# Causal mask in the scan's second term, VectorE's remainders and sums one step later, softmax values loaded three steps later: an encoder layer on one core

## The chip, the core and the metric

The kernel runs on one NeuronCore of a Trainium2 chip. Its engines work side by side and wait for each other by semaphores: TensorE (PE, with its weight loads shown apart as PEld), VectorE (DVE), ScalarE (ACT), GpSimd (POOL), and SyncE (SP), which here issues nearly all transfers between the on-chip memory and HBM. TensorE writes only into eight accumulator banks (PSUM), each 128 rows by 512 float32. The metric is the device time of one execution in microseconds (us).

## What is computed

One layer of an encoder over 2048 positions of width 1024, all in float32: a projection, two kinds of attention with 8 heads of 64 each, an output projection, and a squared-ReLU MLP. The change touches the two attentions only.

```python
# stick-breaking heads: strictly causal
z = einsum(q, k) * scale
strict = s_idx < t_idx
log_beta = log_sigmoid(z)
log_1m_beta = where(strict, log_sigmoid(-z), 0.0)
suffix = cumsum(log_1m_beta, reverse=True) - log_1m_beta
w = where(strict, exp(log_beta + suffix), 0.0)
out = einsum(w, v)
...
# softmax heads: own chunk of 64 and the 8 before it, with a bias by distance
p = softmax(einsum(q, k_band) * scale + bias)
out = einsum(p, v_band)
```

The sequence is stored reversed, so the keys that a query may see stand to its right, and the reverse cumulative sum becomes a running product from left to right.

## The kernel before

The kernel has three stages: projections of the first positions (to about 423 us of the profile), attention (to about 1357 us), and the rest of the output projection and the MLP. To keep TensorE busy in the attention stage, the remaining projections and most of the output projection are fed in between as *filler*: `fill` takes some of their matmuls in each step by a credit. Their results are split and stored by jobs in the list `soon`, which the next step runs as `done` (`stf`, `svf` and `xr` are tiles of such jobs).

**Units and steps.** Positions are cut into four groups g of 512. For g = 3, 2, 1, 0 come first the stick-breaking units `SB(h, g, c)`, head h and key group c from g to 3, then the softmax units `CA(h, g)`. A unit has four steps, one for each block of 128 queries. A unit with c equal to g is *diagonal*: its rows get shorter (512, 384, 256, 128 keys). In step i the loop works on a front unit (scores and weights) and on the unit of eight steps before (LAG), the back unit, whose weights are transposed and multiplied with the values. The names below carry head, groups and block: `p_2_2_3_0` is head 2, g 2, c 3, block 0 of a stick-breaking unit; `v_0_2` has two numbers and is head 0, g 2 of a softmax unit.

**One step, in the order of the code.** TensorE transposes one or two 128-key blocks of the back unit (`wt`); `soft1` of the front unit; `parts` (ScalarE rounds wt to `wth`, VectorE subtracts to get the remainder `wtl`: a float32 product is made of rounded parts); `soft2`; the jobs of `done`; the matmuls of values `acc` with wth and wtl of a block three back (AVLAG); the scores `z` (softmax: `cz`, `ct`) of the next step; filler. In `soft1` of a stick-breaking unit ScalarE makes sigmoid(z) in `b` and sigmoid(-z) in z, VectorE scans z into the running product `p`, and GpSimd multiplies b with p, shifted by one. The scan computes p[j+1] = z[j] * p[j] + second[j]; its second operand is a zero repeated over the row. Scores, transposes share four accumulator banks (`pz`), so a score matmul waits until the scan of an earlier score has read its bank.

**The mask.** In a diagonal unit, a third matmul adds -1e30 to the first 128 score columns where the key is not visible (`identb`, `maskb`, in bf16, 1 LDWEIGHTS and 1 matmul). The sigmoids then give 0 and 1 there.

**End of a head.** `finish` has ScalarE copy one half of the accumulator to `otmp`, VectorE add the other half into `o`; after each second head `keep` splits o into `os` and stores it to `scr_m`.

**Loads.** All go through SP's one queue, in its order. At a unit's first step, q, k and (softmax) the bias of the unit two ahead are issued (AHEAD); a unit's values `v` are issued when its own step 2 comes (VST). A softmax v has two buffers, its bias two, so an issue can wait in SP's queue until the buffer's last reader is done. `fw`, `fv`, `fx` and `ow` are the filler's loads. TensorE's order is that of the code; of the other engines a scheduling layer may move independent instructions, so the built program's order is shown below.

Nearly every row of the profile has line L42, the wrapper through which instructions are handed on; rows are told apart by their tiles.

Of the kernel before, what the change touches and what calls it, by code (L numbers as in the profile page):

```python
# [18 lines left out]
P = 128  # L19
S = 2048  # L20
D = 1024
HD = 64
# [57 lines left out]
def encoder_kernel(ctx, tc, xT, c, g1, g2, w_in, w_rest, gqk, bias, w_o, w1, w2, w_ada, b_ada, out):  # L80
# [20 lines left out]
    def scratch(name, shape, *counts):  # L101
# [12 lines left out]

    ident = cpool.tile([P, P], F32, name="ident")
    make_identity(nc, ident)
    identb = cpool.tile([P, P], BF16, name="identb")
    dve.tensor_copy(identb, ident)
    maskb = cpool.tile([P, P], BF16, name="maskb")
    pool.memset(maskb, 0.0)  # L120
    pool.affine_select(
        out=maskb, in_=maskb, pattern=[[1, P]], base=0, channel_multiplier=-1,
        compare_op=ALU.is_gt, fill=NEG,
    )
    ones = cpool.tile([P, P], F32, name="ones")
    pool.memset(ones, 1.0)
    zero = cpool.tile([P, 1], F32, name="zero")
# [19 lines left out]
    def split(hi, lo, src, lo_eng=None):  # L147
        act.copy(hi, src)
        (lo_eng or dve).tensor_tensor(lo, src, hi.bitcast(F32), op=ALU.subtract)
# [503 lines left out]
    if True:  # L653
# [36 lines left out]
        def finish(u):  # L690
            r = (u.h % 2) * HD
            q = HD - r
            if u.h % 2 == 0:
                pend["o"] = op.tile([P, TB], F32, tag="o", name=f"o{u.nm}")
            o = pend["o"]
            tmp = op.tile([P, TB], F32, tag="otmp", name=f"otmp{u.nm}")
            act.copy(tmp[r : r + HD, :], u.acc[q : q + HD, :])
            dve.tensor_tensor(o[r : r + HD, :], u.acc[r : r + HD, :], tmp[r : r + HD, :], op=ALU.add)
            if u.h % 2:
                soon.append(lambda: keep(u, o))  # L700

        def keep(u, o):

# [9 lines left out]
        class Unit:  # L713
# [13 lines left out]
                    pe.transpose(wt[:, qi * P : (qi + 1) * P], self.weights(qi, kb), ident)  # L727
                self.wt[j] = wt

            def parts(self, j):  # L730
                kb, q0, q1 = self.blocks[j]
                nm = f"{self.nm}_{kb}"
                wt = self.wt[j]
                wh = wtp.tile([P, TB], F32R, tag="wth", name=f"wth{nm}")
                wl = wtp.tile([P, TB], F32R, tag="wtl", name=f"wtl{nm}")
                cols = slice(q0 * P, q1 * P)
                split(wh[:, cols], wl[:, cols], wt[:, cols])
                self.wt[j] = (wh, wl, cols, kb)

            def values(self, j):  # L740
# [10 lines left out]
        class SB(Unit):  # L751
# [21 lines left out]
            def scores(self, qi):  # L773
                nm = f"{self.nm}_{qi}"
                c0 = qi * P if self.diag else 0
                n = TB - c0
                self.z = z = pz.tile([P, TB], F32, tag="z", name=f"z{nm}")
                qs = slice(qi * P, (qi + 1) * P)
                pe.matmul(z[:, :n], self.q[:, 0, qs], self.k[:, c0:], start=True, stop=False)
                pe.matmul(z[:, :n], self.q[:, 1, qs], self.k[:, c0:], start=False, stop=not self.diag)  # L780
                if self.diag:
                    pe.matmul(z[:, :P], identb, maskb, start=False, stop=True)

            def soft1(self, qi):
                nm = f"{self.nm}_{qi}"
                c0 = qi * P if self.diag else 0
                n = TB - c0
                z = self.z
                b = zw.tile([P, TB], F32, tag="w", name=f"b{nm}")
                pt = zp.tile([P, TB + 1], F32, tag="p", name=f"p{nm}")  # L790
                act.activation(b[:, :n], z[:, :n], AF.Sigmoid, scale=0.125)
                act.activation(z[:, :n], z[:, :n], AF.Sigmoid, scale=-0.125)
                before = ones[:, 0:1] if self.diag else self.carry[qi]
                pool.tensor_copy(pt[:, 0:1], before)
                dve.tensor_tensor_scan(
                    pt[:, 1 : n + 1], z[:, :n], zero.to_broadcast([P, n]), 1.0 if self.diag else before,
                    op0=ALU.mult, op1=ALU.add,
                )
                pool.tensor_tensor(b[:, :n], b[:, :n], pt[:, :n], op=ALU.mult)
                self.carry[qi] = pt[:, n : n + 1]  # L800
                self.ws.append((b, c0))
# [304 lines left out]
        weight = STEPS * sum(u.weight for u in units) + LAG * 0.6  # L1106
        credit = 0.0
        rest = 0
        late, soon, first = [], [], []

        def fill(part, more=0):

# [37 lines left out]
        def value(u, j):  # L1150
            u.values(j)

        VST = 2
        AHEAD = 2
        for u in units[:AHEAD]:
            load(u)
# [9 lines left out]
        pado.tile([P, 80], F32, tag="pad", name="pado")  # L1166
        fp = ph.enter_context(tc.tile_pool(name="fp", bufs=3))
        wtp = ph.enter_context(tc.tile_pool(name="wtp", bufs=4))
        ldq = sp
        steps = [(u, st) for u in units for st in range(STEPS)]  # L1170

        turns = {STEPS * n: 4 if u.ca else 8 for n, u in enumerate(units) if n and u.ca != units[n - 1].ca}
        for i in range(len(steps) + LAG):
            if i % STEPS == 0:
                if i // STEPS + AHEAD < len(units):
                    load(units[i // STEPS + AHEAD])
            vi = i - VST
            if vi >= 0 and vi % STEPS == 0 and vi // STEPS < len(units):
                units[vi // STEPS].load_values()
            front, fs = steps[i] if i < len(steps) else (None, 0)  # L1180
            back, bs = steps[i - LAG] if i >= LAG else (None, 0)
            done = list(soon)
# [4 lines left out]
                js = range(nb * bs // STEPS, nb * (bs + 1) // STEPS)  # L1187
            for j in js:
                back.transposes(j)
            if front is not None:  # L1190
                front.soft1(fs)
            while first:
                first.pop(0)()
            for j in js:
                back.parts(j)
                late.append((back, j))
            if front is not None:
                front.soft2(fs)
# [6 lines left out]
                u.scores(st)  # L1205
            fill(front.weight if front else 0.6, turns.get(i, 0))
            later.tick()
        for u, j in late:
            value(u, j)
        while soon:  # L1210
# [526 lines left out]
```

## Time and profile before

| | |
|---|---|
| median of 3 runs | 2654.53 us (2651.93 to 2657.14) |
| profiled execution | 2654.84 us, its span 2653.0 us |
| mean granted TensorE clock | 0.997 |
| transfers | 650.70 MB, mean 245 GB/s |
| scans | 192 of 512 with a carry, 128 in diagonal units |
| remainders wtl | 544 |
| value loads v | 136 of 256 KB, median 4.0 us from issue to landing |

How rows are read: in the views of instructions, "out<-in" names the tiles, then partitions x elements, xcount, busy time in us, mean ns of one, and the engine's idle time before them with who ended it. A timeline row begins with start and duration in us, merges neighbours of one kind (x2), and ends with the idle time before it in brackets. A waiting row says: engine, tile <- the one it waited for: us in total, times, the longest. Matmuls overlap in the pipeline, so their cost is read from start to start and not from their durations.

### The profile page before, as it was taken

What the parts mean: (1) busy time and instruction counts of PE and PEld (TensorE: products, weight loads), DVE (VectorE), ACT (ScalarE), POOL (GpSimd) and SP (SyncE); (2) the same over time, 40 slices, a digit from 0 to 9 for tenths busy, and PEclk for the clock granted to TensorE, in tenths of its full rate; (3) what the DMA queues carried; (4) which work ended last, traced back from release to release, by engine and by line L of the source; (5) the groups of instructions that cost most, each with busy time, mean ns of one, the idle gap of its engine ahead of it and who ended that gap; (6) DMA issues with size and microseconds to landing.
All of it is one profiled execution on the core that took longest, in us unless ns stands there. A gap on an engine that the chain in (4) does not pass through costs nothing. (4 is left out here: it accounts for less than half of the span.)

```text
span 2653.0 us, 39748 instructions
## 1 busy us (share of the span) xinstructions
PE 2589.6 (98%) x12656; PEld 2134.1 (80%) x12656; DVE 1921.2 (72%) x3299; ACT 1510.1 (57%) x2974; POOL 922.3 (35%) x1192
## 2 busy tenths in 40 slices
PE   6999999899999999999999999999999999999999
PEld 5888887778877887787888888878888888888887
DVE  6656766688788888999768777768856656555555
ACT  5333436688788778788655444456544444444443
POOL 4330155466566657777523333100002232200000
PEclk9999999999999999999999999999999999999999
DMA  9879878979976698766677777786665443375574
GB/s 331 304 305 360 328 307 266 283 235 292 282 228 214 223 273 262 247 191 206 210 281 269 262 279 253 258 322 216 244 247 173 150 156 146 140 257 191 194 268 157
DMA packets 257521, 650.70 MB, mean 245 GB/s; under 512 B 29472, under 2 KB 53024, under 8 KB 248224
## 3 DMA queue, kind: packets, MB, share of 16 engines
q1 hardware_dynamic: 256016, 643.45, 70.8%
q10 hardware_dynamic: 1296, 4.72, 0.4%
q8 instruction: 100, 1.64, 0.3%
q14 instruction: 109, 0.89, 0.1%
HBM read 456.69 MB, written 191.37 MB: 244 GB/s over the span
## 5 line engine op out<-in xcount | busy, mean ns | idle before, releaser
L42 PE MATMUL ps<-oph,opv 128*128 128x512 f32 x2688 | 612.4, 389 | 2.0 <-ACT opv L42 1.8
L42 PE MATMUL ps<-h,opw 128*128 128x512 f32 x2664 | 604.5, 389 | 1.0 <-DVE cx L42 1.0
L42 PEld LDWEIGHTS ps<-oph,opv 128*128 128x128 f32 x2688 | 503.9, 188 | 108.5 <-ACT opv L42 2.7
L42 PEld LDWEIGHTS ps<-h,opw 128*128 128x128 f32 x2664 | 500.0, 188 | 105.1 <-DVE cx L42 1.4
L42 POOL TENSOR_TENSOR b<-b,p 128x512 f32<-128x512 f32 (+1 forms) x320 | 360.5, 1127 | 192.0 <-DVE p L42 172.2
L42 DVE TENSOR_TENSOR wtl<-wt,wth 128x512 fp32r<-128x512 f32 (+3 forms) x544 | 290.0, 545 | 38.4 <-ACT wth L42 35.8
L42 DVE TENSOR_TENSOR oph<-hw,oph 128x512 fp32r<-128x512 f32 x224 | 156.6, 699 | 221.7 <-ACT oph L42 221.7
L42 ACT CAST wth<-wt 128x512 fp32r<-128x512 f32 (+3 forms) x544 | 258.8, 486 | 99.1 <-PE wt L42 84.4
L42 ACT CAST oph<-hw 128x512 fp32r<-128x512 f32 x224 | 139.5, 623 | 282.6 <-PE ps L42 266.1
L42 PE MATMUL pt<-w,ht 128*128 128x512 f32 x1248 | 289.0, 391 | 2.2 <-DVE qh L42 2.2
L42 POOL TENSOR_TENSOR ts<-w 128x512 f32<-128x512 f32 x32 | 44.2, 1382 | 664.0 <-DMA w<-in_w_dram 563.3
L42 PEld LDWEIGHTS pt<-w,ht 128*128 128x128 f32 x1248 | 232.8, 188 | 50.9 <-ACT csq L42 2.9
L42 DVE TENSOR_TENSOR_SCAN p<-z,p,zero 128x512 f32<-128x512 f32 x192 | 245.9, 1281 | 36.2 <-ACT z L42 32.6
L42 PE MATMUL acc<-wth,v 128*128 128x512 f32 (+3 forms) x544 | 221.3, 411 | 5.0 <-DMA v<-scr_v 5.0
L42 ACT ACTIVATE b<-z 128x512 f32<-128x512 f32 (+1 forms) x320 | 171.8, 537 | 56.6 <-PE z L42 40.7
L42 PE MATMUL z<-k,q 128*128 128x512 f32 (+3 forms) x640 | 187.4, 374 | 15.2 <-DVE p L42 13.6
L42 POOL TENSOR_TENSOR e<-e,cols 128x640 f32<-128x640 f32 (+4 forms) x128 | 143.3, 1123 | 136.4 <-DVE cols L42 91.4
L42 PE MATMUL acc<-wtl,v 128*128 128x512 f32 (+3 forms) x544 | 186.0, 348 | 0.0
L42 DVE TENSOR_TENSOR opw<-w,opw 128x512 fp32r<-128x512 f32 x127 | 98.2, 775 | 112.5 <-ACT opw L42 112.4
L42 PE MATMUL wt<-ident,b 128*128 128x128 f32 x1088 | 171.6, 273 | 1.2 <-DVE p L42 0.7
L42 ACT ACTIVATE z<-z 128x512 f32<-128x512 f32 (+1 forms) x320 | 170.6, 533 | 0.0
L42 PEld LDWEIGHTS wt<-ident,b 128*128 128x128 f32 x1088 | 135.7, 140 | 41.7 <-DVE p L42 2.0
(197 smaller groups left out, 4220.5 us busy)
## 6 DMA issues: line engine op xcount, KB each, us to landing
hw<-scr_hid SPq DMA_DIRECT2D x112, 512.0 KB, 4.1
k<-scr_k SPq DMA_DIRECT2D x272, 128.0 KB, 4.5
v<-scr_v SPq DMA_DIRECT2D x136, 256.0 KB, 4.0
q<-scr_q SPq DMA_DIRECT2D x128, 256.0 KB, 5.1
w<-in_w_dram SPq DMA_DIRECT2D x64, 512.0 KB, 5.4
hw<-scr_s SPq DMA_DIRECT2D x64, 512.0 KB, 4.6
wa<-in_w_ada_dram SPq DMA_DIRECT2D x48, 512.0 KB, 6.7
ow<-scr_wo SPq DMA_DIRECT2D x24, 1024.0 KB, 6.2
```

What stands on the lines that cost most here:

```text
L42: return lambda *x, **y: self.tc.keep_in_program_order(f(*x, **y))
```

## The change

1. The mask's matmul and its weight load are gone, and `identb` and `maskb` with them. In a diagonal unit the scan's second operand is now the tile `diagonal`, an identity of 128 columns followed by zeros, and it starts at 0 in place of 1: the product stays 0 until the query's own column, is set to 1 there by the second term, and runs on from it. Weights left of it are multiplied by 0. The tile is made once, on GpSimd, at the begin of the attention stage.
2. The remainder wtl of a step's last block is issued at the begin of the next step (`rests`), ahead of its scan; the sum into o one step later than before.
3. Values of softmax units are issued 5 steps after the unit's first and not 2; those of stick-breaking units stay at 2.

```diff
+            def add():
+                dve.tensor_tensor(o[r : r + HD, :], u.acc[r : r + HD, :], tmp[r : r + HD, :], op=ALU.add)
+                if u.h % 2:
+                    soon.append(lambda: keep(u, o))
+            soon.append(add)
-            dve.tensor_tensor(o[r : r + HD, :], u.acc[r : r + HD, :], tmp[r : r + HD, :], op=ALU.add)
-            if u.h % 2:
-                soon.append(lambda: keep(u, o))
...
-            def parts(self, j):
+            def parts(self, j, behind):
...
-                split(wh[:, cols], wl[:, cols], wt[:, cols])
+                act.copy(wh[:, cols], wt[:, cols])
+                rests.append(
+                    lambda: dve.tensor_tensor(wl[:, cols], wt[:, cols], wh[:, cols].bitcast(F32), op=ALU.subtract)
+                )
+                if not behind:
+                    rests.pop()()
...
-                pe.matmul(z[:, :n], self.q[:, 1, qs], self.k[:, c0:], start=False, stop=not self.diag)
-                if self.diag:
-                    pe.matmul(z[:, :P], identb, maskb, start=False, stop=True)
+                pe.matmul(z[:, :n], self.q[:, 1, qs], self.k[:, c0:], start=False, stop=True)
...
-                before = ones[:, 0:1] if self.diag else self.carry[qi]
+                before, begin = (zero, diagonal[:, :n]) if self.diag else (self.carry[qi], zero.to_broadcast([P, n]))
                 pool.tensor_copy(pt[:, 0:1], before)
                 dve.tensor_tensor_scan(
-                    pt[:, 1 : n + 1], z[:, :n], zero.to_broadcast([P, n]), 1.0 if self.diag else before,
+                    pt[:, 1 : n + 1], z[:, :n], begin, 0.0 if self.diag else before,
                     op0=ALU.mult, op1=ALU.add,
                 )
...
-        VST = 2
+        VST = (2, 5)
...
+        diagonal = dgp.tile([P, TB], F32, name="diagonal")
+        pool.memset(diagonal[:, P:], 0.0)
+        pool.tensor_copy(diagonal[:, :P], ident)
...
-            vi = i - VST
-            if vi >= 0 and vi % STEPS == 0 and vi // STEPS < len(units):
-                units[vi // STEPS].load_values()
+            for ca, lead in enumerate(VST):
+                n, at = divmod(i - lead, STEPS)
+                if at == 0 and 0 <= n < len(units) and units[n].ca == ca:
+                    units[n].load_values()
...
             for j in js:
                 back.transposes(j)
+            while rests:
+                rests.pop(0)()
             if front is not None:
                 front.soft1(fs)
...
             for j in js:
-                back.parts(j)
+                back.parts(j, j == js[-1])
```

What the built programs' orders show of it, engine by engine:

VectorE, before, in the second group, where head 2's scans run and the filler's values (svf) are split:

```order
L42 SCALAR_TENSOR_TENSOR p_2_2_3_0_6074<-z_2_2_3_0_6062,p_2_2_2_0_5975,zero 128x512
L42 TENSOR_TENSOR wtl_1_2_3_3_6081<-wt_1_2_3_3_6068,wth_1_2_3_3_6080 128x512
L42 TENSOR_TENSOR svf_10_2_0_5814<-pf_10_3_5826,svf_10_2_0_5814 128x4x64
L42 TENSOR_TENSOR svf_10_2_1_5815<-pf_10_3_5826,svf_10_2_1_5815 128x4x64
L42 SCALAR_TENSOR_TENSOR p_2_2_3_1_6107<-z_2_2_3_1_6092,p_2_2_2_1_6000,zero 128x512
```

VectorE, after, at the same place (the scans have their name from the instruction's kind):

```order
L42 SCALAR_TENSOR_TENSOR p_2_2_3_0_6028<-z_2_2_3_0_6015,p_2_2_2_0_5933,zero 128x512
L42 TENSOR_TENSOR o_0_2_3_6009<-acc_0_2_2_5806,otmp_0_2_3_6010 64x512
L42 TENSOR_TENSOR svf_10_2_0_5773<-pf_10_3_5784,svf_10_2_0_5773 128x4x64
L42 TENSOR_TENSOR svf_10_2_1_5774<-pf_10_3_5784,svf_10_2_1_5774 128x4x64
L42 TENSOR_TENSOR wtl_1_2_3_3_6035<-wt_1_2_3_3_6021,wth_1_2_3_3_6034 128x512
L42 SCALAR_TENSOR_TENSOR p_2_2_3_1_6062<-z_2_2_3_1_6046,p_2_2_2_1_5957,zero 128x512
```

The remainder moved behind the two svf, and the sum o, which stood ahead of the first scan shown, moved behind it.

SP's queue, before, at the first softmax head of the second group:

```order
L826 DMA bias_2_7272<-scr_b_236 128x640
L684 DMA v_0_2_7324<-scr_v_2_0_152 128x512
L684 DMA v_0_2_7324<-scr_v_3_0_154 128x512
L226 DMA scr_k_0_0_108<-stf_2_0_7362 128x2x512
L943 DMA fw_3_0_7382<-scr_w_223 128x2048
L667 DMA q_3_2_7388<-scr_q_2_1_101 64x1024 x2
L675 DMA k_3_2_7391<-scr_k_2_1_133 64x512 x2
L675 DMA k_3_2_7391<-scr_k_3_1_137 64x512 x2
L826 DMA bias_2_7396<-scr_b_237 128x640
L684 DMA v_1_2_7448<-scr_v_2_0_152 128x512
```

The same, after:

```order
L827 DMA bias_2_7206<-scr_b_236 128x640
L218 DMA scr_k_0_0_108<-stf_2_0_7292 128x2x512
L944 DMA fw_3_0_7312<-scr_w_223 128x2048
L659 DMA q_3_2_7318<-scr_q_2_1_101 64x1024 x2
L667 DMA k_3_2_7321<-scr_k_2_1_133 64x512 x2
L667 DMA k_3_2_7321<-scr_k_3_1_137 64x512 x2
L827 DMA bias_2_7326<-scr_b_237 128x640
L676 DMA v_0_2_7355<-scr_v_2_0_152 128x512
L676 DMA v_0_2_7355<-scr_v_3_0_154 128x512
L944 DMA fw_3_1_7405<-scr_w_223 128x2048
```

The values v_0_2 moved behind a store, a weight load of 1 MB, and q, k and bias of head 3.

SP's queue, before, at the sixth head of that group, and below it the same after:

```order
L952 DMA fw_4_4_8067<-scr_wv_224 128x2048
L684 DMA v_5_2_8074<-scr_v_2_1_153 128x512
L684 DMA v_5_2_8074<-scr_v_3_1_155 128x512
L667 DMA q_0_1_8148<-scr_q_1_0_80 64x1024 x2
L675 DMA k_0_1_1_8151<-scr_k_1_0_112 64x512 x2
L952 DMA fw_4_6_8190<-scr_wv_224 128x2048
L684 DMA v_6_2_8226<-scr_v_2_1_153 128x512
```

```order
L953 DMA fw_4_4_8001<-scr_wv_224 128x2048
L659 DMA q_0_1_8079<-scr_q_1_0_80 64x1024 x2
L667 DMA k_0_1_1_8082<-scr_k_1_0_112 64x512 x2
L953 DMA fw_4_6_8121<-scr_wv_224 128x2048
L676 DMA v_5_2_8124<-scr_v_2_1_153 128x512
L676 DMA v_5_2_8124<-scr_v_3_1_155 128x512
```

Here v_5_2 moved behind the next unit's q and k and a second weight load of 1 MB. In the first group, v_0_3 and those after it likewise stand behind the bias of the unit three ahead. TensorE's order is the same but for the mask's 128 weight loads and 128 matmuls.

More of the change, by code (lines that the diff above doesn't have):

```diff
@@ L116, in encoder_kernel @@
     make_identity(nc, ident)
[L117 to L124, printed above, removed]
     ones = cpool.tile([P, P], F32, name="ones")
@@ L1108, in encoder_kernel @@
         rest = 0
-        late, soon, first = [], [], []
+        late, soon, first, rests = [], [], [], []
         def fill(part, more=0):
@@ L1168, in encoder_kernel @@
         wtp = ph.enter_context(tc.tile_pool(name="wtp", bufs=4))
+        dgp = ph.enter_context(tc.tile_pool(name="dgp", bufs=1))
+        diagonal = dgp.tile([P, TB], F32, name="diagonal")
+        pool.memset(diagonal[:, P:], 0.0)
+        pool.tensor_copy(diagonal[:, :P], ident)
         ldq = sp
@@ L1207, in encoder_kernel @@
             later.tick()
+        while rests:
+            rests.pop(0)()
         for u, j in late:
```

## The prediction

> **What bounds the kernel now.** I read the busy times first, then the engines' times by stage, then who waits for whom in the stage that the change touches, and last the rows around single steps.
>
> ```profile
> PE 2589.6 (98%) x12656; PEld 2134.1 (80%) x12656; DVE 1921.2 (72%) x3299; ACT 1510.1 (57%) x2974; POOL 922.3 (35%) x1192
> ```
>
> TensorE is the bound over the whole. The three stages (projections, attention, MLP), by the view of stretches (PE, PEld, DVE, ACT, POOL busy, then granted clock, DMA share, GB/s):
>
> ```profile
> 0.00:423.00 423.00, 399.56 (x1826) 330.79 (x1826) 273.44 (x463) 166.08 (x302) 120.65 (x231) 1.00 0.85 318
> 423.00:1357.00 934.00, 901.64 (x5142) 738.50 (x5142) 789.94 (x1572) 728.08 (x1600) 604.58 (x822) 0.99 0.78 241
> 1357.00:2653.00 1296.00, 1288.41 (x5691) 1064.82 (x5689) 857.81 (x1265) 615.98 (x1073) 197.11 (x139) 1.00 0.63 224
> ```
>
> All edits lie in the middle stage. There PE is idle for 934.0 - 901.6 = 32.4 us, so waits removed can give 32 us at most, and work taken from PE gives its own length as long as nothing else fills it. The waits of that stage (total, times, longest):
>
> ```profile
> POOL b L42 <- DVE p L42: 172.2, 190, 20.0
> DVE o L42 <- ACT otmp L42: 26.5, 37, 1.4
> ACT svf L42 <- DVE svf L42: 16.5, 12, 1.6
> PE z L42 <- DVE p L42: 13.6, 27, 1.5
> PE acc L42 <- DMA v<-scr_v: 5.0, 2, 4.1
> PE cz L42 <- DMA k<-scr_k: 3.3, 2, 2.2
> ```
>
> PE waits for a free score bank (z, held until its scan p is done), and in four places for a load. The rows for o and svf are VectorE and ScalarE waiting for each other.
>
> **The mask's matmuls** go: 128 of them, with their weight loads. First their group, then the rows around one, then a step that has none.
>
> ```profile
> L42 PE MATMUL z<-maskb,identb 128*128 128x128 bf16 x128 | 29.4, 230 | 0.0
> ```
>
> ```profile
> 1203.52 0.23 PE L42 MATMUL z<-maskb,identb 128*128 128x128 bf16 x1
> 1203.56 0.71 PE L42 MATMUL po<-fx,ow 128*128 128x512 f32 x2
> 1204.10 0.60 PE L42 MATMUL wt<-ident,b 128*128 128x128 f32 x4
> ...
> 1205.47 0.62 PE L42 MATMUL po<-fx,ow 128*128 128x512 f32 x2
> 1205.93 0.27 PE L42 MATMUL wt<-ident,b 128*128 128x128 f32 x1
> ```
>
> From the mask's start to the transposes 1204.10 - 1203.52 = 0.58 us pass with two po; without it two po take 1205.93 - 1205.47 = 0.46. One mask costs 0.12 us of PE's time, and 128 of them 15.4 us. The bounds are 0.04 (mask to the next start), 5.1 us in all, and the whole 0.23, 29.4 us. I take 0.12, since it counts the slower start of the next matmul too.
>
> The Trainium skill, "TensorE: Matmul & The Clock Gate", section "Wait — 56ns, not 53.3ns?", gives 55.6 ns from start to start for a warm matmul of 128 columns. By it the masks would be worth 128 x 0.0556 = 7.1 us, an estimate, and the sum below would come out 7 us higher. The row is more than twice that; its neighbours are of another type, and the page measures matmuls of one kind in a row.
>
> Is PE's saved time filled by VectorE? The busiest late stretch, and VectorE's costs:
>
> ```profile
> 1140.00:1256.00 116.00, 114.95 (x634) 93.42 (x632) 106.98 (x132) 97.42 (x195) 89.65 (x129) 1.00 0.59 190
> ```
>
> ```profile
> L42 DVE TENSOR_TENSOR_SCAN p<-z,p,zero 128x512 f32<-128x512 f32 x192 | 245.9, 1281 | 36.2 <-ACT z L42 32.6
> L42 DVE TENSOR_TENSOR wtl<-wt,wth 128x512 fp32r<-128x512 f32 (+3 forms) x544 | 290.0, 545 | 38.4 <-ACT wth L42 35.8
> ```
>
> ```profile
> L42 DVE TENSOR_TENSOR_SCAN p<-z,zero x128: 400/812/1229, 425.0 to 1235.6; 128x512 f32<-128x512 f32 x32, 128x384 f32<-128x384 f32 x32, 128x256 f32<-128x256 f32 x32, 128x128 f32<-128x128 f32 x32
> ```
>
> VectorE is at 92% there, PE at 99%. The masks are 15.4 of 934 us, 1.6%, less than VectorE's 8% of air; and the diagonal's scans, median 812 ns, leave it more room in just the steps that get shorter than the 1281 ns of the others. I take nine tenths: **-14 us**. The scan's second term becomes a stored tile in place of a repeated zero. No row shows that form; the longest diagonal scan is 1229 ns and the carried one 1281, so I take no change, with 0.05 us either way (128 x 0.05 = 6 us of VectorE, under its air). The tile's clear and copy on POOL stand ahead of the first scan and wait for a projection weight's buffer; POOL's longest wait for a scan, 20.0 us in the rows of waits, is the one before its first product, so I take nothing. The 128 first-column copies only read another constant.
>
> **VectorE's order.** The last remainder (wtl) of a step and the head's sum (o) come a step later. Without other work between, the cyclic order scan, wtl, scan stays. With filler evictions (svf) between, they now go ahead of wtl, and ScalarE's second svf copy, which waited 12 times for VectorE, starts one wtl (0.545 us) earlier: 12 x 0.545 = 6.5 us. A later wtl is covered, as its matmul runs two or three steps behind. The o that waited 37 times for its copy no longer holds the next scan; but that scan mostly waits for ScalarE's z anyway, and o still takes its turn one scan later, so I take nothing for it. PE sees only part: **-3 us**, half of 6.5. Ends: -13.6 (all score-bank waits) and +3 (the same amount lost, because wtl now delays scans and banks).
>
> **Values of the softmax heads three steps later.** In SP's queue each such load falls behind the next unit's q, k and bias, sometimes behind a 1 MB weight load. Three places count. First the first head of the first group, by issues, landings (of the v, then the bias) and PE's waits:
>
> ```profile
> 481.09 0.55 SPq L684 DMA_DIRECT2D v<-scr_v  x1
> 485.97 0.33 SPq L826 DMA_DIRECT2D bias<-scr_b  x1
> 491.93 0.76 PE L42 MATMUL acc<-wth,v 128*128 128x512 f32 x1 [4.10 <-DMA v<-scr_v]
> 494.24 1.19 PE L42 MATMUL cz<-k,q 128*128 128x512 f32 x2 [1.12 <-DMA k<-scr_k]
> ```
>
> ```profile
> DMA to landing us min/median/max: 10.7/10.7/10.7
> ```
>
> ```profile
> DMA to landing us min/median/max: 8.5/8.5/8.5
> ```
>
> The v landed at 491.8, the bias at 494.5; transfers land in the order of issue. Behind the bias, v lands near 494.5: the wait grows by 2.7 us, and the 1.1 us for k right behind it goes. The second head repeats it with the 2.2 us wait for k in exchange. I take **+2 us** (0 to +4).
>
> Then the first head of the second group (v, weight, bias; landing of v, of bias; PE's first use):
>
> ```profile
> 658.32 0.92 SPq L684 DMA_DIRECT2D v<-scr_v  x2
> 661.33 1.07 SPq L943 DMA_DIRECT2D fw<-scr_w  x1
> 666.87 0.33 SPq L826 DMA_DIRECT2D bias<-scr_b  x1
> ```
>
> ```profile
> DMA to landing us min/median/max: 5.9/6.0/6.1
> ```
>
> ```profile
> DMA to landing us min/median/max: 9.1/9.1/9.1
> ```
>
> ```profile
> 672.66 0.39 PE L42 MATMUL acc<-wth,v 128*128 128x512 f32 x1
> ```
>
> It landed at 664.3 and 664.9, far ahead of its use. Behind the bias, which landed at 676.0, less the 1.2 us of its own two transfers and plus 0.6 for the first, it lands at 675.4: **+2.7 us** where there was no wait (0 to +4).
>
> Third, the sixth head of that group, where v falls behind q, k and a weight load of 1 MB:
>
> ```profile
> 714.90 0.79 SPq L684 DMA_DIRECT2D v<-scr_v  x2
> 721.63 0.33 SPq L952 DMA_DIRECT2D fw<-scr_wv  x1
> 726.12 0.47 PE L42 MATMUL acc<-wth,v 128*128 128x512 f32 x1 [0.87 <-DMA v<-scr_v]
> ```
>
> ```profile
> DMA to landing us min/median/max: 11.1/11.4/11.8
> ```
>
> ```profile
> DMA to landing us min/median/max: 10.5/10.5/10.5
> ```
>
> That weight landed at 732.1. Less v's two transfers (2.1) and plus one (1.0), v lands at 731, 5 us late. But the loads ahead no longer stand behind a blocked v, which shortens the queue: **+3 us** (0 to +5). The remaining heads had a margin of some us: **+1** (-1 to +3).
>
> What the move gives is in SP's queue:
>
> ```profile
> SPq L684 <- PE acc L42: 121.6, 44, 6.6
> ```
>
> SP stood 121.6 us at value loads whose buffer was still in use, with everything behind them. PE saw of this only the 3.3 us for k, counted above.
>
> **Sum.** The profiled execution took 2654.8 us (span 2653.0, 1.8 around it), 0.3 above the median of the runs. 2654.8 - 14 - 3 + 2 + 2.7 + 3 + 1 = 2646.5 us.
>
> **Rivals.** (1) The loads are hidden all the same, since SP no longer blocks: the +8.7 of values falls away and the k waits' 3.3 us come in: 2646.5 - 8.7 - 3.3 = 2634.5. For it: 121.6 us of blocked queue. Against: the three chains above. (2) VectorE becomes the bound in the stick-breaking stretches, and only a third of the masks' 15.4 us is kept, with no gain from the order: 2654.8 - 5 + 8.7 = 2658.5, or about 2650 if the values are hidden; for it the 92%, against it the air in diagonal steps. (3) Slower: late values cost clock as well as time. Around the 4.10 us wait the granted clock is:
>
> ```profile
> 486.00:510.00 24.00, 16.57 (x79) 13.35 (x78) 11.42 (x43) 11.30 (x35) 8.10 (x11) 0.79 0.98 307
> ```
>
> That is 0.21 x 24 = 5 us of full-speed time. If the second and third places reach waits of that kind, each adds about 5 us and its upper end: 2646.5 + 10 + 1.3 + 2 = 2660, slower by just over 0.2%. It decides from about 4 us of wait, the length of the only wait in the stage with such a clock. The Trainium skill, "TensorE: Matmul & The Clock Gate", section "What's actually happening", has the array fall to half rate after an idle window of about 3.4 us; the 4.10 us row agrees, and by that rule 2.7 us at the second place would cost nothing more, 5 at the third would. (4) The new scan form is slower and takes the gain back: with the 1281 of the carried form for every diagonal scan, 128 x (1.28 - 0.81) = 60 us more of VectorE, about 2670; only if its cost no longer went by its width.
>
> **How the numbers follow.** This kernel's measurement tells about 0.2%, 5.3 us, from no change. Forecast 0.45 (own range 2640 to 2652, four fifths of it faster by more than that), rival 1 0.25 (faster), rival 2 0.17 (same, at times slower), the masks at the page's price 0.03 (2653.5, same), rival 3 0.08, rival 4 0.02. Faster: 0.36 + 0.25 = 0.61; slower: 0.02 of rival 2, 0.08 and 0.02 = 0.12; same 0.27. The range runs from rival 1 to between rival 2's two values: 2634 to 2657.
>
> **What would show it.** In the profile after: no mask group; PE busy in the middle stage about 15 us less (29 at most); the DVE row for otmp near zero; PE's wait for v up from 5.0 to about 13, in three or four places, and that for k gone; SP's wait at value loads well below 121.6; the diagonal scan's median still near 812. I am wrong if the wait for v does not grow, if PE's waits for scans rise by as much as the masks gave, or if the clock falls around a second head.

## The result and the profile after

The changed kernel is slower: 2667.64 us median of 6 runs (2663.12 to 2675.03) against 2654.03 (2651.93 to 2657.14) for the kernel before, ratio 1.0054, 95% interval 1.0038 to 1.0071. That is 14 us more (10 to 19), where 2646.5 was predicted and 2634 to 2657 given as the range. The profiled execution of the changed kernel is the longest of its six, 2675.0 us, so its rows hold some 7 us more than its median run; sizes are therefore taken from the runs, places and causes from the rows.

Busy times after, then the three stages (PE, PEld, DVE, ACT, POOL busy, granted clock, DMA share, GB/s):

```profile
PE 2586.8 (97%) x12528; PEld 2135.8 (80%) x12528; DVE 1927.0 (72%) x3298; ACT 1508.4 (56%) x2974; POOL 924.0 (35%) x1192
```

```profile
0.00:423.00 423.00, 398.16 (x1822) 329.45 (x1823) 273.94 (x462) 165.50 (x301) 120.16 (x228) 1.00 0.84 317
423.00:1377.00 954.00, 899.55 (x5025) 741.17 (x5024) 791.32 (x1572) 728.65 (x1601) 605.05 (x826) 0.99 0.77 237
1377.00:2673.00 1296.00, 1289.10 (x5685) 1065.14 (x5683) 861.73 (x1264) 614.22 (x1072) 198.74 (x139) 1.00 0.63 224
```

The first and the last stage are as they were. The middle one took 954 us in place of 934. PE lost its 128 masks, but is busy there only 2 us less (899.6 after 901.6) and idle 54 us where it was idle 32. So most of the time went into waits, but not all. With only the masks gone (the first run below) PE is busy 893.3 us in this stage, 8 less than before. In the changed kernel it is 6 more than that, and the granted clock was lower in two stretches, around the softmax heads of the first two groups. Before, and below it after:

```profile
423.00:560.00 137.00, 123.77 (x702) 99.21 (x702) 101.75 (x241) 103.18 (x269) 80.62 (x131) 0.96 0.87 268
660.00:760.00 100.00, 97.39 (x576) 81.14 (x574) 79.76 (x239) 74.49 (x172) 54.34 (x55) 1.00 0.87 266
```

```profile
423.00:560.00 137.00, 114.34 (x618) 93.32 (x617) 93.03 (x228) 96.16 (x250) 74.87 (x123) 0.94 0.87 259
660.00:760.00 100.00, 86.90 (x496) 73.39 (x495) 66.60 (x229) 61.65 (x140) 44.90 (x38) 0.95 0.87 257
```

That is 0.02 x 137 + 0.05 x 100 = 7.7 us of full-speed time lost to the clock, an estimate from these rows and at most so much, as PE also stood idle in part of it. The waiting rows of the changed kernel that matter:

```profile
PE acc L42 <- DMA v<-scr_v: 19.9, 5, 9.5
...
PE wt L42 <- DVE wtl L42: 15.4, 23, 1.5
...
ACT svf L42 <- DVE svf L42: 13.6, 12, 1.7
...
PE z L42 <- DVE p L42: 11.2, 29, 1.4
...
DVE o L42 <- ACT otmp L42: 1.0, 1, 1.0
```

Two rows carry the loss in waits: PE's wait for values v, 5.0 before and 19.9 now, and a wait that was 0.6 us in 2 places before: transposes (wt) that stand until VectorE has done a remainder (wtl), 15.4 us in 23 places. The row for o and otmp fell from 26.5 to 1.0 as the sums came later, and PE's wait for k, 3.3 us before, is gone; the two rows above outweigh both. SP's queue did not come free:

```profile
SPq L676 <- PE acc L42: 117.3, 40, 6.3
```

It still stands 117.3 us at value loads, where it stood 121.6. The scan with the stored tile costs what it cost with the repeated zero, 398/812/1227 ns after 400/812/1229:

```profile
L42 DVE TENSOR_TENSOR_SCAN p<-z,diagonal x128: 398/812/1227, 426.1 to 1256.4; 128x512 f32<-128x512 f32 x32, 128x384 f32<-128x384 f32 x32, 128x256 f32<-128x256 f32 x32, 128x128 f32<-128x128 f32 x32
```

### The profile page after: what moved, and what is told of

It reads as the page before. It is cut to its first block, busy times and chain, and to the rows that moved or that the text cites. A ratio compares the mean times of both kernels' runs of the same rounds, so it can differ in the third digit from the quotient of the medians.

```text
span 2673.2 us, 39502 instructions
## 1 busy us (share of the span) xinstructions
PE 2586.8 (97%) x12528; PEld 2135.8 (80%) x12528; DVE 1927.0 (72%) x3298; ACT 1508.4 (56%) x2974; POOL 924.0 (35%) x1192
## 5 line engine op out<-in xcount | busy, mean ns | idle before, releaser
L42 PE MATMUL acc<-wth,v 128*128 128x512 f32 (+3 forms) x544 | 222.6, 413 | 21.0 <-DMA v<-scr_v 19.9
L42 PE MATMUL wt<-ident,b 128*128 128x128 f32 x1088 | 172.8, 274 | 11.7 <-DVE wtl L42 10.6
```

The lines of the kernel that those rows point to most:

```text
L42: return lambda *x, **y: self.tc.keep_in_program_order(f(*x, **y))
```

## The experiments

All ratios are against the kernel before, run on the same chip. The theories first were: A, each of the three edits has a price of its own; B, the time freed by the masks cannot be had, since VectorE sets the steps, and all of the loss is that of the values.

### Each edit alone, and two together

The masks alone; remainders, sums and values as before:

```diff
-                pe.matmul(z[:, :n], self.q[:, 1, qs], self.k[:, c0:], start=False, stop=not self.diag)
-                if self.diag:
-                    pe.matmul(z[:, :P], identb, maskb, start=False, stop=True)
+                pe.matmul(z[:, :n], self.q[:, 1, qs], self.k[:, c0:], start=False, stop=True)
...
+                before, begin = (zero, diagonal[:, :n]) if self.diag else (self.carry[qi], zero.to_broadcast([P, n]))
```

> The mask edit alone: second term in the scan, no mask matmuls; VectorE's order and the value loads as before. Theory A (each edit has its own price; the masks' 15.4 us of PE are real, and the two moves cost more than they give): 8 to 15 us faster than before, PE's waits for scans and loads as before within 5 us. Theory B (the masks' time cannot be had, since VectorE sets the steps; all of the loss is the value loads): within 3 us of before, with PE's score-bank waits up by about 10 us.

Measured: 2648.93 us, ratio 0.9982 (0.9973 to 0.9991), 5 us faster.

The values alone:

```diff
-        VST = 2
+        VST = (2, 5)
```

> The softmax heads' values three steps later, alone. Theory A: 8 to 15 us slower than before, PE's wait for v near 15 us in about 5 places in place of 5.0 in 2, k waits gone, a second stretch of half clock in the second group. Theory B: 13 us slower, the whole of the change's loss, likewise from waits for v.

Measured: 2667.47 us, 1.0060 (1.0049 to 1.0072), 13.5 us slower by the medians, 16 by the ratio.

The remainders and sums a step later alone, with the masks' matmuls:

```diff
+            soon.append(add)
...
+                rests.append(
+                    lambda: dve.tensor_tensor(wl[:, cols], wt[:, cols], wh[:, cols].bitcast(F32), op=ALU.subtract)
+                )
```

> The remainders and the sums one step later, alone; masks and value loads as before. Theory A: 5 to 12 us slower, PE's wait of the transposes for wtl up from 0.6 to 10 us or more, since filler splits and sums now stand ahead of the remainder that frees a score bank. Theory B: within 3 us of before; the 15.4 us of such waits seen after the change are the masks' saved time, turned into a wait.

Measured: 2661.80 us, 1.0030 (1.0019 to 1.0042), 7.8 us slower.

Masks and order, values as before (against the changed kernel):

```diff
-        VST = (2, 5)
+        VST = (2, 2)
```

> The whole change but with the value loads as before (mask and order). Theory A: the sum of the two alone, from 8 us faster to 2 us slower, with the transposes' wait for wtl near 15 us. Theory B: within 3 us of before.

Measured: 2657.72 us, 1.0016 (1.0007 to 1.0024), 3.7 us slower.

The edits nearly add up: -5.1 + 7.8 + 13.5 = +16.2 against +13.6 for all three. A holds in that each has its price; its size for the masks (8 us or more) does not. B is wrong on the order, which costs by itself. The values' rows, PE's first use of each late v, in the run with that edit alone:

```profile
493.53 0.77 PE L42 MATMUL acc<-wth,v 128*128 128x512 f32 x1 [8.52 <-DMA v<-scr_v]
509.73 0.47 PE L42 MATMUL acc<-wth,v 128*128 128x512 f32 x1 [0.93 <-DMA v<-scr_v]
516.69 0.47 PE L42 MATMUL acc<-wth,v 128*128 128x512 f32 x1 [1.19 <-DMA v<-scr_v]
674.63 0.47 PE L42 MATMUL acc<-wth,v 128*128 128x512 f32 x1 [1.68 <-DMA v<-scr_v]
697.71 0.47 PE L42 MATMUL acc<-wth,v 128*128 128x512 f32 x1 [1.69 <-DMA v<-scr_v]
733.36 0.56 PE L42 MATMUL acc<-wth,v 128*128 128x512 f32 x1 [4.19 <-DMA v<-scr_v]
```

These six are 18.2 us: the first, third and fourth head of the first group and the first, third and sixth of the second. Three of them (493.53, 674.63 and 733.36) are places that the prediction named. The second head of the first group, which it named too, waits 1.71 us; the view puts that down to ScalarE, but its v was issued at 492.80 and landed 10.1 us later, at 502.9, just ahead of this row:

```profile
503.09 0.47 PE L42 MATMUL acc<-wth,v 128*128 128x512 f32 x1 [1.71 <-ACT e L42]
```

The rows are not the whole price. The six runs with this edit have a mean granted clock of 0.994 to 0.997, on average 0.995, and the six of the changed kernel 0.994 to 0.996, likewise 0.995; the 23 runs of the kernel before beside them have 0.996 to 0.998, on average 0.997. A difference of 0.002 in 2654 us is up to 5 us, an estimate from these clocks and an upper end, since PE also waits in a part of that time.

### Values: the later step, or the place in the queue?

The kernel before, with softmax values two steps later, but issued ahead of the q, k and bias of that step:

```diff
-        VST = 2
+        VST = (2, 4)
...
+            for ca, lead in enumerate(VST):
+                ...
             if i % STEPS == 0:
                 if i // STEPS + AHEAD < len(units):
                     load(units[i // STEPS + AHEAD])
-            vi = i - VST
-            ...
```

> The kernel before with the softmax values two steps later, not three, and issued ahead of the loads of the unit two ahead (q, k, bias), not behind them; mask and VectorE's order as before. Values three steps later and behind those loads gave 2667.5 us, the kernel before 2654.0. Theory A (the place in the queue, behind bias, q, k and a weight, is the cost): 2654 to 2658 us, TensorE's wait for v 5 to 9 us. Theory B (the later issue itself is the cost, whatever stands ahead): two thirds of the loss, 2661 to 2665 us, wait for v 12 us or more.

Measured: 2655.82 us, 1.0005 (0.9997 to 1.0014). Its waits for v:

```profile
491.88 0.77 PE L42 MATMUL acc<-wth,v 128*128 128x512 f32 x1 [5.18 <-DMA v<-scr_v]
727.18 0.47 PE L42 MATMUL acc<-wth,v 128*128 128x512 f32 x1 [1.01 <-DMA v<-scr_v]
```

Theory A: two steps' delay cost nothing that can be told, 1.3 us, as long as v is not behind the next unit's loads. One step more, and behind them, costs 13.5. The one step and the place were not parted further. The granted clock of its eleven runs is 0.997 on average, as before.

### Order: the sums or the remainders?

Against masks with both later: the remainders back in their place, so that only the sums are later; then the sums back, so that only the remainders are.

```diff
-                rests.append(
-                    lambda: dve.tensor_tensor(wl[:, cols], wt[:, cols], wh[:, cols].bitcast(F32), op=ALU.subtract)
-                )
+                split(wh[:, cols], wl[:, cols], wt[:, cols])
```

> The mask edit with the sums o a step later, remainders and values as before; to be held against the mask edit alone (2648.9 us). Theory A (the later remainder is the cost of the order edit, since it holds the bank that the transposes two steps on need): the remainders stay where they were, so 2646 to 2650 us, TensorE's wait of transposes for wtl stays under 2 us, and VectorE's row for otmp (26.5 us) falls near zero. Theory B (the sum, now standing between scan and remainder work, is what delays it): 2653 to 2657 us, as with both.

Measured: 2661.68 us, 1.0034 (1.0022 to 1.0047).

```diff
-            soon.append(add)
+            add()
```

> The mask edit with the remainders a step later, sums and values as before; against the mask edit alone (2648.9 us) and the mask with both (2657.7 us). Theory A (late remainders hold the transposes' bank, since the filler's evictions svf and xr now go ahead of them on VectorE): 2654 to 2658 us, transposes' wait for wtl 8 to 15 us. Theory B (the sums do it): 2647 to 2650 us and that wait under 3 us.

Measured: 2660.97 us, 1.0028 (1.0019 to 1.0037).

Both theories fell. Over the masks alone, one half costs 12.8 us, the other 12.0, and both together 8.8. I matched the matmuls of two traces one by one, in the attention stage, and summed how much longer the time from one start to the next became, by what the second of the two writes (all others: what lies inside a run of like matmuls, too):

| us, difference to masks alone | before z | before ct | before wt | before cz | all others | sum |
|---|---|---|---|---|---|---|
| sums later | +14.9 | 0.0 | -2.4 | -4.5 | -1.8 | +6.2 |
| remainders later | -5.4 | +14.7 | +7.0 | -6.6 | -0.9 | +8.8 |
| both later | -2.9 | -0.7 | +13.9 | -6.2 | +1.0 | +5.1 |

(Single profiled runs; the sums are some us below what the runs say.) By the intervals of the three runs, both together are only just told apart from the sums alone, and hardly from the remainders alone. The later sum frees the softmax steps (before cz), and in a stick-breaking step it comes ahead of the scan, whose bank the next scores need. VectorE's sum and scan there, and PE's scores that wait for that scan:

```profile
818.62 0.69 DVE L42 TENSOR_TENSOR o<-acc,otmp 64x512 f32<-64x512 f32 x1
...
819.35 0.96 DVE L42 TENSOR_TENSOR_SCAN p<-z,diagonal 128x384 f32<-128x384 f32 x1
...
820.36 0.44 PE L42 MATMUL z<-k,q 128*128 128x128 f32 x2 [0.71 <-DVE p L42]
```

A later remainder with the sum in its old place stands behind a sum that waits 1.66 us for ScalarE's copy, and holds the bank that the scores ct need:

```profile
973.12 0.69 DVE L42 TENSOR_TENSOR o<-acc,otmp 64x512 f32<-64x512 f32 x1 [1.66 <-ACT otmp L42]
...
974.52 0.55 DVE L42 TENSOR_TENSOR wtl<-wt,wth 128x384 fp32r<-128x384 f32 x1
...
975.12 1.11 PE L42 MATMUL ct<-k,q 128*128 128x128 f32 x8 [1.25 <-DVE wtl L42]
```

Putting off the sum too takes that away: before ct 14.7 us more become 0.7 less. Why the 14.9 us before z are gone as well with both later, these rows do not show. What remains then is the third pattern, in the changed kernel: sum, remainder, and a transpose that waits.

```profile
929.15 0.69 DVE L42 TENSOR_TENSOR o<-acc,otmp 64x512 f32<-64x512 f32 x1
...
929.88 0.69 DVE L42 TENSOR_TENSOR wtl<-wt,wth 128x512 fp32r<-128x512 f32 x1
...
930.63 0.66 PE L42 MATMUL wt<-ident,b 128*128 128x128 f32 x4 [0.93 <-DVE wtl L42]
```

### Is it the bank?

First try: the remainder is made from `wth` alone (it becomes zero), so that it no longer reads the bank; as it is, with the masks' edit, and with masks and order.

```diff
-                split(wh[:, cols], wl[:, cols], wt[:, cols])
+                act.copy(wh[:, cols], wt[:, cols])
+                dve.tensor_tensor(wl[:, cols], wh[:, cols].bitcast(F32), wh[:, cols].bitcast(F32), op=ALU.subtract)
```

> The kernel before, but the remainder wtl is made from the rounded part alone (wth - wth, so it is zero): it no longer reads the transposes' bank, which is then free after ScalarE's copy. A base for the next two runs. Theory A (remainders hold banks that TensorE waits for): 2640 to 2652 us. Theory B (in the old order they hold nothing that is waited for, the row of transposes for wtl is only 0.6 us): 2652 to 2656 us. A changed length of that instruction would be seen in its row.

> The same zero remainder, with the mask edit. Theory A (of the 0.11 us that a mask takes in place, half is lost since VectorE's work holds score banks, so more comes through with banks free earlier): 8 to 12 us below the run with the zero remainder alone. Theory B (the loss has another place, loads or the engine's own spacing): 4 to 6 us below it, as the masks gave without this.

> The same zero remainder, with the mask edit and with remainders and sums a step later. With true remainders this order cost 8.8 us over the mask alone. Theory A (all of that, and more, was the transposes' bank held by the late remainder: the gaps ahead of wt grew by 15 us, while gaps in the softmax steps shrank by 8): 3 to 10 us below the run with zero remainder and mask. Theory B (the late remainder costs by its place on VectorE or by its late matmul): 6 to 10 us above it.

Measured: 2712.33 us, 1.0223 (1.0209 to 1.0237); 2709.63, 1.0213 (1.0199 to 1.0227); 2719.19, 1.0243 (1.0229 to 1.0257). The three say nothing on the bank, since the instruction itself became longer (the row is of the first of the three):

```profile
L42 DVE TENSOR_TENSOR wtl<-wth 128x512 fp32r<-128x512 f32 (+3 forms) x544 | 434.7, 813 | 11.1 <-ACT wth L42 10.7
```

It took 434.7 us where `wtl<-wt,wth` took 290.0 (mean 545 ns), 145 us more on VectorE, and the kernel became 58 us longer. What they show is a VectorE that is nearly full, busy 93% of the attention stage (919.8 of 986 us, 423 to 1409 us of the first run) where it was 85%: there the masks are worth 2.7 us, inside the intervals, and the order still costs 9.6 us with no bank held by a remainder, though on so full an engine this does not carry over.

Second try: remainders in their old place, and at the place of the late one only a copy of one column, from the bank (`wt`) or from SBUF (`wth`).

```diff
                 split(wh[:, cols], wl[:, cols], wt[:, cols])
+                if behind:
+                    rests.append(lambda: dve.tensor_copy(touch, wt[:, cols][:, 0:1]))
```

> The mask edit with remainders, sums and values in their old places, and one added VectorE instruction at the place to which the late remainder went: a copy of one column of the transposes' bank into a scratch column. It holds that bank as long as a late remainder would, and takes little time itself. Theory A (the late remainder costs by the bank it holds): 6 to 12 us above the next run, which has the same instruction without the bank, about 2657 to 2664 us, and TensorE's waits of transposes and ct on VectorE return, 10 us or more. Theory B (it costs by its length among VectorE's work, or by the matmul that needs it): within 3 us of the next run.

Measured: 2663.41 us, 1.0031 (1.0019 to 1.0043).

> The same added copy of one column at the same place, but from wth in SBUF, so that no bank is held. Theory A and B alike: the mask edit alone (2648.9 us) plus what some 500 short instructions cost VectorE, 0 to 6 us: 2649 to 2655 us, and no waits of transposes on VectorE beyond those of the mask alone.

Measured: 2658.09 us, 1.0011 (1.0002 to 1.0020). This one's copies and its wait of transposes for them, and then that wait in the run that holds the bank:

```profile
L42 DVE COPY touch<-wth 128x1 f32<-128x1 f32 x448 | 64.1, 143 | 0.8
```

```profile
PE wt L42 <- DVE touch L42: 0.5, 2, 0.3
```

```profile
PE wt L42 <- DVE touch L42: 11.1, 26, 0.9
```

With the same VectorE work, holding the bank to that place costs 5.3 us (some 1 to 9, from the two intervals). That is under theory A's 6 to 12 and over B's 3: the bank is a part of what a late remainder costs, by the medians less than half of the 12.0 us that remainders alone cost, at the upper end of the interval most of it. What makes up the rest was not parted. In the matched traces the gaps before ct and wt grow by 18.8 us, and about as much is given back in the other gaps, so a waiting row here is far more than its price. The traces carry the 5.3 us only from 560 us on, where the sum over all gaps is 5.3; from 423 to 560 it is -5.3, and there the profiled run without the bank, the longest of its twelve, had the lower clock (0.91 after 0.96 from 423 to 500 us). The copies themselves cost 8 us (ratio 1.0011 against 0.9982), more than the 6 I allowed, though the intervals reach 6: 64 us more of VectorE in 448 short pieces.

### What a mask costs

The kernel before with each mask issued twice:

```diff
+                    pe.matmul(z[:, :P], identb, maskb, start=False, stop=False)
                     pe.matmul(z[:, :P], identb, maskb, start=False, stop=True)
```

> The kernel before with each mask matmul issued twice (the second adds the same mask once more): 128 more bf16 weight loads and matmuls. Theory A (a mask costs 0.08 to 0.12 us of TensorE's time in place, and its removal gave only 5 us because VectorE's scans and the loads took part back): 9 to 14 us slower, 2663 to 2668 us, and TensorE's wait for scans smaller than the 13.6 us before. Theory B (a mask costs TensorE only the 0.04 us between its start and the next start): 5 us slower, 2659 us.

Measured: 2658.44 us, 1.0016 (1.0007 to 1.0025), 4 us slower, in the kernel's time theory B. The rows at the place of the prediction's example (po is a matmul of the filler):

```profile
1203.84 0.33 PE L42 MATMUL z<-k,q 128*128 128x128 f32 x2
1204.02 0.28 PE L42 MATMUL z<-maskb,identb 128*128 128x128 bf16 x2
1204.11 0.71 PE L42 MATMUL po<-fx,ow 128*128 128x512 f32 x2
1204.66 0.60 PE L42 MATMUL wt<-ident,b 128*128 128x128 f32 x4
```

From the scores' start to the transposes 1204.66 - 1203.84 = 0.82 us pass, with one mask it was 1204.10 - 1203.34 = 0.76. Over all masks without a wait nearby, the second adds 56 ns (median from the first mask's start to the next matmul 95 ns, 39 with one). The Trainium skill, "TensorE: Matmul & The Clock Gate", section "Wait — 56ns, not 53.3ns?", has 55.6 ns; for the second mask, one of two alike in a row, the trace agrees. So in place the second mask costs more than theory B's 0.04 us, 128 x 0.056 = 7.2 us in all, and by the medians not all of that reaches the kernel's time. The first one, between matmuls of another type, saved more: from the last score matmul to the second matmul after it the medians fall by 73, 119, 116 and 127 ns for diagonal blocks of 128, 256, 384 and 512 columns in the run with the masks' edit alone.

### The better version

Sums later in the softmax heads only, on top of the masks, and then only in the first six softmax heads of a group:

```diff
+            if u.ca and u.h < 6:
+                soon.append(add)
+            else:
+                add()
```

> The mask edit, and the sums o a step later in the softmax heads only; in the stick-breaking heads the sums, and everywhere the remainders and values, stay as before. Against the mask edit alone (2648.9 us) and the mask with all sums later (2661.7). Theory A (a later sum frees the softmax steps, about 8 us by the gaps after ct that shrink, and harms only the stick-breaking steps, about 15 us by the gaps ahead of z that grow): 2639 to 2645 us. Theory B (what the sums free in the softmax steps is waited for at the next load or scan): 2647 to 2652 us.

Measured (without `u.h < 6`): 2645.95 us, 0.9972 (0.9962 to 0.9983).

> The mask edit, with sums a step later in the softmax heads 0 to 5 alone; the last two heads of each group, whose ends lie beside stick-breaking steps, keep theirs. Against sums later in all softmax heads (2646.0 us). Theory A (a later sum helps only where no scan follows): 2642 to 2645 us, the gaps ahead of z at 533 to 558 us no longer wider. Theory B (what is freed is waited for at the group's loads): 2645 to 2649 us.

Measured: 2644.76 us, 0.9956 (0.9943 to 0.9969): 12 us faster than before (8 to 15), the fastest version here. Its interval overlaps with that of the run above, so the two are not told apart; against the masks alone (0.9973 to 0.9991) the first is not told apart either, the second is. The first lies between A and B, the second at the edge of A. Both theories have a part: in the matched traces, against masks alone, the gaps before z are 3.2 us wider with all softmax sums later and 1.2 with six heads', and those before cz 4.0 narrower, but 3.7 come back at the values. In the trace of the faster one the waiting rows for scans and sums:

```profile
PE z L42 <- DVE p L42: 16.8, 30, 1.5
...
DVE o L42 <- ACT otmp L42: 9.6, 17, 1.4
```

The scans' wait stays near the 16.2 us of the masks alone, and the sums' is down from 26.1.

## Why the prediction was wrong

**The masks: the price was near, the nine tenths were wrong.** In place a mask gave back 0.07 to 0.13 us by the width of its block, and around the masks the matched traces save 11.9 us, where 0.12 each had made 15.4. But 8.5 came back elsewhere in the stage, 4.2 of it before the first scores of a step, where the wait for a scan's bank falls. The waiting row of the run with the masks' edit alone:

```profile
PE z L42 <- DVE p L42: 16.2, 29, 1.5
```

That row was 13.6. The term measured 5.1 (2.4 to 7.2) and not 14. The failed step is "less than VectorE's 8% of air": that air (idle time) is a mean over steps, while a score matmul waits for one scan. That 64 us of short copies cost 8 us fits this. It is not all of it: 5.4 of the 8.5 us came back before 500 us, among the first loads, where the run with the masks' edit alone also had the lower clock. Before, and below it in that run:

```profile
423.00:500.00 77.00, 68.32 (x398) 54.56 (x397) 55.86 (x124) 56.38 (x149) 45.15 (x79) 0.96 0.95 298
```

```profile
423.00:500.00 77.00, 67.60 (x356) 55.37 (x356) 54.78 (x123) 54.44 (x144) 46.21 (x80) 0.91 0.97 290
```

How much of the shortfall is VectorE's and how much is loads and clock was not parted. Rival 2 had the size, "only a third of the masks' 15.4 us"; its cause, VectorE as the bound, is shown only in part. The sum by the Trainium skill's figure, 7 us higher, was nearer, but by luck: a mask in place gave back more than that figure, and a part of it returned as waits.

**The scan's form and the tile's clear: right.** 812 ns as before, and the first diagonal scan starts at 426.1 after 425.0.

**VectorE's order: wrong in sign.** Forecast -3, measured +7.8 alone, and beyond the end of +3 that the prediction kept for it. The step that failed is "A later wtl is covered, as its matmul runs two or three steps behind". The matmul is covered (the changed kernel's PE waits 0.1 us before all acc<-wtl), but the remainder is also the last reader of its bank, which the transposes and ct want sooner. "wtl now delays scans and banks" stood there as an end of the range, and its price was taken no higher than a lost svf gain. The step that was to gain, ScalarE's wait for svf, gave 2.9 us (16.5 to 13.6) and not 6.5, and "I take nothing" for the sums missed both their gain in softmax steps and their loss in stick-breaking ones.

**Values: the named places right, the others too small.** Forecast +8.7, measured +13.5 (13 to 19). By rows, v's wait grew by 18.2 - 5.0 = 13.2 us, the second head's 1.7 came in and k's 3.3 went, net 11.6. The first two heads gave 8.52 - 4.10 + 1.71 - 3.3 = 2.8 us where +2 was taken, the second place 1.7 for +2.7, the third 4.19 - 0.87 = 3.3 for +3. The mis-sized term is "The remaining heads", +1: the rows at 509.73, 516.69 and 697.71 are 3.8 us. The profiled run, the fastest of its six and at a clock of 0.997, is 10.6 us above the profiled run of before, as the rows say. The rest of the 13.5 is in the other runs; their lower clock, which the sum put at nothing, is the likely place, but no trace of them was kept. The claim that the loads ahead would no longer stand behind a blocked v fell: 117.3 us of SP's wait are left.

**The rival on the other side.** Rival 3 asked for waits over about 4 us at the second and third place and 5 us of clock at each. In the changed kernel the waits for v are these; the one at 684.88 is the prediction's second place, and though the view names ScalarE, its first v, issued at 679.1, landed 5.7 us later, at 684.7:

```profile
501.45 0.77 PE L42 MATMUL acc<-wth,v 128*128 128x512 f32 x1 [9.46 <-DMA v<-scr_v]
512.47 0.53 PE L42 MATMUL acc<-wth,v 128*128 128x512 f32 x1 [2.02 <-DMA v<-scr_v]
684.88 0.47 PE L42 MATMUL acc<-wth,v 128*128 128x512 f32 x1 [1.14 <-ACT e L42]
697.22 0.77 PE L42 MATMUL acc<-wth,v 128*128 128x512 f32 x1 [0.44 <-DMA v<-scr_v]
710.93 0.47 PE L42 MATMUL acc<-wth,v 128*128 128x512 f32 x1 [1.98 <-DMA v<-scr_v]
748.32 0.77 PE L42 MATMUL acc<-wth,v 128*128 128x512 f32 x1 [5.95 <-DMA v<-scr_v]
```

Clock around the first, the wait at 697.22 and the last of them:

```profile
486.00:510.00 24.00, 13.68 (x70) 11.32 (x68) 9.43 (x33) 10.06 (x29) 8.11 (x10) 0.79 1.01 309
690.00:702.00 12.00, 10.10 (x51) 8.38 (x51) 7.82 (x27) 6.55 (x15) 5.77 (x5) 0.86 0.89 236
742.00:766.00 24.00, 17.25 (x92) 14.33 (x91) 11.38 (x32) 13.49 (x33) 9.75 (x12) 0.86 0.68 213
```

At the sixth head of the second group the clock fell as that rival said, 0.14 x 24 = 3.4 us; at the first place it was 0.79 before too. The Trainium skill's window of about 3.4 us ("TensorE: Matmul & The Clock Gate", "What's actually happening") agrees with the last row: 5.95 us have a lower clock behind them. The middle row does not fit it: no wait of PE from 690 to 702 us is longer than 1.5 us, and the clock was 0.86. So shorter waits can have a lower clock behind them too, and "from about 4 us of wait" was too high a bar. The mechanism was there, at up to 5 us by the clocks of the runs, and is the smaller part of the loss. The prediction missed by 21.1 us, of which the masks are 8.9, the order 10.8 and the values 4.8, less 2.6 by which the edits overlap and 0.8 by which the profiled run of before stood above its median. All three terms erred to the same side.

## What to carry to other kernels

Before an instruction is put off, ask what it holds besides its result: the last reader of a shared accumulator bank sets when the next writer starts, however late its own consumer is. Work that fits into an engine's mean idle time can still land ahead of the one scan that a matmul waits for, so move it only in those steps where nothing of that chain follows (here the sums of the softmax heads). And put a load off together with its place in the queue in view: two steps later and ahead of the next unit's loads cost nothing that could be told here, three steps later and behind them 13.5 us, though which of the two did it was not parted.

## What the runs showed of the hardware

A subtraction with both operands in SBUF is not always as fast as one with an operand in PSUM. The two rows, before and with the zero remainder (min/median/max ns):

```profile
L42 DVE TENSOR_TENSOR wtl<-wt,wth x544: 262/657/693, 434.2 to 1354.8; 128x512 fp32r<-128x512 f32 x94, 128x128 fp32r<-128x128 f32 x37, 128x256 fp32r<-128x256 f32 x27, 128x384 fp32r<-128x384 f32 x24
```

```profile
L42 DVE TENSOR_TENSOR wtl<-wth x544: 255/673/1787, 431.7 to 1405.6; 128x512 fp32r<-128x512 f32 x94, 128x128 fp32r<-128x128 f32 x37, 128x256 fp32r<-128x256 f32 x27, 128x384 fp32r<-128x384 f32 x24
```

The median is nearly the same and the longest 1.1 us longer, about the length of one of GpSimd's products (mean 1127 ns in the profile before). The Trainium skill, "SBUF — State Buffer", section "Who interferes with whom", says that a VectorE instruction with two SBUF inputs contends with a GpSimd instruction that reads SBUF, for a port pair that only one of them holds at a time. The rows agree with it: GpSimd's busy time rose as well, from 922.3 to 1062.9 us. No run here took GpSimd's work away to show it alone.
